# Moving the two additions behind each Strassen group of the down projection from GpSimd to VectorE, in a decoder block on one core

## The chip, the cores and the metric

The kernel runs on one core of one Trainium2 chip. The metric is the device time of one execution in microseconds (us); lower is better. The kernel before has a median of 2799.49 us over three runs.

## The reference

The reference is one decoder layer on 512 tokens of width 2048 in float32: a sparse-attention and pooling mixer, a 4-head cross-attention into 256 memory tokens, and a dense SwiGLU feed-forward network, each between two normalisations. The change touches only the last part:

```python
h = rms_norm(x, ln_ffn_pre[l])
y = (jax.nn.silu(h @ w_gate[l]) * (h @ w_up[l])) @ w_down[l]
x = x + rms_norm(y, ln_ffn_post[l])
```

The hidden width of the network is 5632, that is 44 blocks of 128 rows; `w_down` brings them back to 2048 columns.

## The kernel before

**Precision by splitting.** Every float32 matrix product is made of three TensorE products: an operand x is split in a rounded part hi (ScalarE, L96) and a rest lo = x - hi (VectorE, L97), and `mm3` multiplies hi by hi (L112), hi by lo (L113) and lo by hi (L114). Each weight block thus goes through a pipeline before TensorE can use it: a DMA issued by SyncE into a ring of 4 buffers `wraw`, then the split into a ring of 3 buffers `whi` and one of 3 buffers `wlo`. A `wraw` buffer is free for the next DMA when L97 has read it; a `wlo` buffer when TensorE has used it.

**The down projection.** The output y is held transposed, as 16 tiles `ys` of 128 rows by 512 tokens in SBUF. The 44 blocks of the hidden width are taken in slices. For s = 0 and s = 1 there is a plain slice of 4 blocks (function `down`, whose results are copied into `ys` by ScalarE at L1050 or added to it by VectorE at L1052), and then a slice of 12 blocks that is multiplied by Strassen's method. A last plain slice follows (`half0`, `half1`), and the final normalisation and output.

**A Strassen group.** For each s, eight groups j = 0 to 7 are made, and group j gives the two row tiles `ys[j]` and `ys[j + 8]`. A group calls `strassen` with six sources of 4 x 128 weight columns. For each source, SyncE issues the load (L947), VectorE makes two of the sums of weight blocks (L948: 128 columns, L949: 256 columns), GpSimd makes a third (L950: 128 columns), ScalarE makes `whi` (L96, 896 columns) and VectorE `wlo` (L97, 896 columns). TensorE then makes seven products of 256 columns, three matmuls each: 21 matmuls for a source, 126 for a group. The product into `psO` comes first for every source but a group's first, so a late `wlo` shows at L114 of `psO`. When the six sources are done, ScalarE copies `psO` (L961) and VectorE makes the four result sums from PSUM into the tile `e` (L963, L964 and L965 with 512 columns, L966 with 256).

**Behind the group** stand the two additions of the change, at L1063: 512 columns of `e` each, added to `ys[j]` and to `ys[j + 8]`, with all operands in SBUF. At j = 3 the activations of the next plain slice are loaded and split (two or more L97 of 512 columns on VectorE), ordered behind the last VectorE and ScalarE instruction traced so far (L1059). After the eighth group, `late` takes the last VectorE and ScalarE instruction; the splits of the Strassen operands of s = 1 are ordered behind it (L1054).

**Order.** Each engine runs its instructions in the order in which they are written into its queue. The order is made by a planner before the kernel runs: it plays the program on its own cost model, and takes at each step the ready instruction with the highest priority. Loads and weight preparation (L947 to L951) carry a priority 1000 ahead of their place in the program, the additions at L1063 carry none. Another engine for an instruction can therefore change the order of others.

**The same pattern without GpSimd.** The gate and up projection (f = 4 to 43) uses the same function `strassen` with eight sources for a group. Behind each group VectorE makes two multiplications of 512 columns (`swiglu`, L877 and L879) with both operands in SBUF.

Of the kernel before, what the change touches and what calls it, by code (L numbers as in the profile page):

```python
# [13 lines left out]
ALU = mybir.AluOpType  # L14
# [855 lines left out]
def ffn(net, xctx, xs, xt0, yctx, ys, rb, rf, x2T, second, close):  # L870
    tc, nc, a = net.tc, net.nc, net.a
# [99 lines left out]
    for f in range(NPLAIN, NF):  # L971
        e = strassen(fe, [a["w_gu"][f, j] for j in range(hp)], xops)
# [4 lines left out]
    def act_tile(pool, pair, f, early=EARLY):  # L977
        x0 = pool.tile([P, S], F32, name="a1", bufs=2) if pool is fl else pool.tile([P, 2 * S], F32, name="as", bufs=2)
        x0 = x0[:, :S]
        with tc.high_priority(early):  # L980
            nc.sync.dma_start(x0, actT[f])
            net.split(*pair, x0)
        return pair
# [9 lines left out]
    ys = [fp.tile([P, S], F32, name=f"y{j}") for j in range(KD)]  # L993
# [13 lines left out]
    def operands(i, f):  # L1007

        x = fs.tile([P, 4, 256], F32, name="as", bufs=2)
        nc.sync.dma_start(x[:, 2:4], actT[f].rearrange("p (b c) -> p b c", b=2))  # L1010
        nc.sync.dma_start(x[:, 0:2], actT[f + 1].rearrange("p (b c) -> p b c", b=2))
        net.split(*xq[i], x[:, 0:3])
        t = fs.tile([P, 4, 256], F32, name="t")
        nc.vector.tensor_tensor(t[:, 0:2], x[:, 3:4].broadcast_to([P, 2, 256]), x[:, 1:3], op=ALU.subtract)
        nc.vector.tensor_tensor(t[:, 2], x[:, 1], t[:, 1], op=ALU.subtract)
        nc.vector.tensor_tensor(t[:, 3], x[:, 0], t[:, 2], op=ALU.subtract)
        for k in range(2):
            net.split(tq[i][0][k], tq[i][1][k], t[:, 2 * k:2 * k + 2])
        b = [tuple(v[:, k] for v in xq[i]) for k in (2, 0, 1)]
        return (*b, *[(tq[i][0][k // 2][:, k % 2], tq[i][1][k // 2][:, k % 2]) for k in (1, 2, 0, 3)])  # L1020
# [11 lines left out]
    def down(s, c, act):  # L1032

        ps = [net.psum(("GGSS", "TTSO")[c % 2][d]) for d in range(4)]

        def add(part):
            for f, hi, lo in part:
                for d in range(4):
                    sl = slice(d * P, (d + 1) * P)
                    net.mm3(ps[d], hi[:, sl], lo[:, sl], *act[f], f == 0, f == len(act) - 1)  # L1040
        gemm512(s, c, len(act), [[i] for i in range(len(act) // 2)], add)
        return ps

    f0, late = 0, []
    for s in range(2):
        for c in range(nb):
            for d, ps in enumerate(down(s, c, act)):
                y = ys[4 * c + d]
                if s == 0:
                    nc.scalar.copy(y, ps)  # L1050
                else:
                    nc.vector.tensor_tensor(y, y, ps, op=ALU.add)  # L1052
        f0 += PL
        with net.behind(late):  # L1054
            ops = [operands(i, f0 + 2 * i) for i in range(NS // 2)]
        f0 += NS
        for j in range(hp):
            if j == 3:
                with net.behind(net.last(nc.vector, nc.scalar)):  # L1059
                    act = [act_tile(fs, p, f0 + i, 0) for i, p in enumerate(plain_at)]  # L1060
            e = strassen(fs, [a["w_dst"][s, j, i] for i in range(NS // 2)], ops)
            for k, o in ((j, 0), (j + hp, 5)):
                nc.gpsimd.tensor_tensor(ys[k], ys[k], e[:, o * 256:(o + 2) * 256], op=ALU.add)  # L1063
        late = net.last(nc.vector, nc.scalar)
    sctx.close()

# [47 lines left out]
    for blocks in ((0, 1), (2,), (3,)):  # L1114
        k0, k1 = 4 * blocks[0], 4 * blocks[-1] + 4
        for i, ps in enumerate(half0(2, blocks, act)):
            for j in range(2):
                k = k0 + 2 * i + j
# [53 lines left out]
def body(tc, a):  # L1172
    a = dict(a)
    for n in ("w_cmp", "w_qk", "w_u", "w_z", "w_mix", "w_xq"):
        a[n] = _Halves(a[n])
    for n in ("w_brp", "w_bra"):
        a[n] = _Whole(a[n])
    a["w_down"] = _Down([a[f"w_down{i}"] for i in range(len(SLICES))])
    with ExitStack() as ctx:
        net = Net(ctx, tc, a)  # L1180
        mctx, ms = sublayer1(net)
        st = sublayer2(net, mctx, ms)
        ffn(net, *st)
# [111 lines left out]
```

## Time and profile before

| | us |
|---|---|
| median of three runs | 2799.49 (2798.63 to 2800.45) |
| the profiled execution, its time | 2799.45 |
| the profiled execution, its span in the trace | 2797.7 |
| TensorE busy | 2741.7 (98%) |
| VectorE busy | 2011.7 (72%) |
| GpSimd busy | 612.8 (22%) |

The span runs from the first to the last instruction; the device time is 1.75 us longer. Busy shares are averages over stages with different limits, and the end of a matmul is modelled, so a stop of TensorE is read from the start times of its instructions.

### The profile page before, as it was taken

What the parts mean: (1) busy time and instruction counts of PE and PEld (TensorE: products, weight loads), DVE (VectorE), ACT (ScalarE), POOL (GpSimd) and SP (SyncE); (2) the same over time, 40 slices, a digit from 0 to 9 for tenths busy, and PEclk for the clock granted to TensorE, in tenths of its full rate; (3) what the DMA queues carried; (4) which work ended last, traced back from release to release, by engine and by line L of the source; (5) the groups of instructions that cost most, each with busy time, mean ns of one, the idle gap of its engine ahead of it and who ended that gap; (6) DMA issues with size and microseconds to landing.
All of it is one profiled execution on the core that took longest, in us unless ns stands there. A gap on an engine that the chain in (4) does not pass through costs nothing.

```text
span 2797.7 us, 48879 instructions
## 1 busy us (share of the span) xinstructions
PE 2741.7 (98%) x18384; PEld 2517.8 (90%) x18384; DVE 2011.7 (72%) x3752; ACT 1252.1 (45%) x2061; POOL 612.8 (22%) x715
## 2 busy tenths in 40 slices
PE   9999999999999999999999999999999999999998
PEld 7788887888878889999989999999999999989996
DVE  5655656565645445777798888888988888899756
ACT  4333545454533235654764444444444444343353
POOL 0000000000000000010333444444224223525303
PEclk9999999999999999999999999999999999999999
DMA  6434332333336456763564444444444453444474
GB/s 186 117 101 131 99 96 78 97 97 109 96 105 200 146 154 213 240 214 121 166 203 128 121 118 120 119 121 120 122 115 125 117 170 105 119 136 106 150 247 165
DMA packets 168493, 384.16 MB, mean 137 GB/s; under 512 B 19312, under 2 KB 39840, under 8 KB 168128
## 3 DMA queue, kind: packets, MB, share of 16 engines
q1 hardware_dynamic: 158816, 352.39, 42.1%
q0 software_dynamic: 8864, 27.60, 3.0%
q8 instruction: 144, 2.36, 0.4%
q10 hardware_dynamic: 576, 1.05, 0.1%
q14 instruction: 93, 0.76, 0.1%
HBM read 343.32 MB, written 37.64 MB: 136 GB/s over the span
## 4 chain that ended last, share of the span: by engine, by line
PE 78%; DVE 12%; DMA 6%; issue 2%; ACT 1%; POOL 0%; DVEq 0%; SPq 0%; POOLq 0%; ACTq 0%
PE psG L112 15%; PE psG L114 15%; PE psG L113 15%; DVE wlo L97 5%; PE psS L112 4%; PE psS L113 4%; PE psS L114 4%; PE psT L112 3%; PE psT L114 3%; PE psT L113 3%; DMA wraw<-in_w_dst_dram 3%; DMA wraw<-in_w_gu_dram 2%; PE psO L114 2%; PE psO L112 2%; PE psO L113 2%
## 5 line engine op out<-in xcount | busy, mean ns | idle before, releaser
L96 ACT CAST whi<-wraw 128x896 fp32r<-128x896 f32 (+2 forms) x773 | 758.3, 984 | 1064.1 <-PE psT L114 340.8
L97 DVE TENSOR_TENSOR wlo<-wraw,whi 128x896 fp32r<-128x896 f32 (+2 forms) x773 | 907.4, 1175 | 263.8 <-ACT whi L96 261.0
L950 POOL TENSOR_TENSOR wraw<-wraw 128x128 f32<-128x128 f32 x416 | 415.6, 1001 | 676.1 <-DVE wraw L949 546.9
L112 PE MATMUL psG<-xh,whi 128*128 128x512 f32 (+1 forms) x1072 | 401.0, 374 | 1.6 <-ACT whi L96 1.5
L114 PE MATMUL psG<-xh,wlo 128*128 128x512 f32 (+1 forms) x1072 | 400.1, 373 | 0.8 <-DVE wlo L97 0.8
L113 PE MATMUL psG<-xl,whi 128*128 128x512 f32 (+1 forms) x1072 | 399.7, 373 | 0.0
L112 PEld LDWEIGHTS psG<-xh,whi 128*128 128x128 f32 x1072 | 203.1, 189 | 35.6 <-ACT whi L96 2.9
L114 PEld LDWEIGHTS psG<-xh,wlo 128*128 128x128 f32 x1072 | 202.4, 189 | 33.9 <-DVE wlo L97 1.0
L113 PEld LDWEIGHTS psG<-xl,whi 128*128 128x128 f32 x1072 | 202.8, 189 | 32.5
L948 DVE TENSOR_TENSOR wraw<-wraw 128x128 f32<-128x128 f32 x416 | 137.8, 331 | 103.2 <-DMA wraw<-in_w_gu_dram 67.3
L949 DVE TENSOR_TENSOR wraw<-wraw 128x256 f32<-128x256 f32 x416 | 185.6, 447 | 6.8
L112 PE MATMUL psT<-th,whi 128*128 128x256 f32 x640 | 179.4, 280 | 0.0
L113 PE MATMUL psT<-tl,whi 128*128 128x256 f32 x640 | 178.8, 279 | 0.0
L114 PE MATMUL psT<-th,wlo 128*128 128x256 f32 x640 | 178.7, 279 | 0.0
L114 PE MATMUL psG<-x,wlo 128*128 128x256 f32 (+1 forms) x544 | 158.1, 291 | 3.3 <-DVE wlo L97 3.3
L112 PE MATMUL psG<-x,whi 128*128 128x256 f32 (+1 forms) x544 | 156.8, 288 | 1.5 <-ACT z L764 1.5
L113 PE MATMUL psG<-x,whi 128*128 128x256 f32 (+1 forms) x544 | 157.5, 290 | 0.0
L112 PE MATMUL psG<-mh,whi 128*128 128x256 f32 x512 | 143.4, 281 | 1.1 <-ACT y L630 1.1
L113 PE MATMUL psG<-ml,whi 128*128 128x256 f32 x512 | 143.1, 280 | 0.0
L114 PE MATMUL psG<-mh,wlo 128*128 128x256 f32 x512 | 142.7, 281 | 0.0
L112 PE MATMUL psS<-xh,whi 128*128 128x256 f32 x480 | 134.8, 281 | 1.4 <-ACT xh L99 1.4
L113 PE MATMUL psS<-xl,whi 128*128 128x256 f32 x480 | 135.0, 282 | 0.9 <-DVE xl L100 0.9
(482 smaller groups left out, 7297.2 us busy)
## 6 DMA issues: line engine op xcount, KB each, us to landing
wraw<-in_w_gu_dram SPq DMA_DIRECT2D x320, 256.0 KB, 2.7
wraw<-in_w_z_dram SPq DMA_DIRECT2D x64, 512.0 KB, 3.8
wraw<-in_w_mix_dram SPq DMA_DIRECT2D x64, 512.0 KB, 4.5
wraw<-in_w_down_dram SPq DMA_DIRECT2D x61, 512.0 KB, 5.3
wraw<-in_w_dst_dram SPq DMA_DIRECT2D x96, 256.0 KB, 2.7
wraw<-in_w_gu_dram SPq DMA_DIRECT2D x29, 512.0 KB, 3.7
wraw<-in_w_qk_dram SPq DMA_DIRECT2D x24, 512.0 KB, 3.6
actT<-zs POOLq DMA_DIRECT2D x40, 256.0 KB, 2.3
```

The source lines that it names most:

```text
L96: nc.scalar.copy(hi, x)
L97: nc.vector.tensor_tensor(lo, x, hi.bitcast(F32), op=ALU.subtract)
L112: mm(ps, lh, rh, start=start, stop=False)
L113: mm(ps, lh, rl, start=False, stop=False)
L114: mm(ps, ll, rh, start=False, stop=stop)
L948: nc.vector.tensor_tensor(u[:, 4], u[:, 0], u[:, 3], op=ALU.add)
L949: nc.vector.tensor_tensor(u[:, 5:7], u[:, 0:5:4], u[:, 1:2].broadcast_to([P, 2, P]), op=ALU.subtract)
L950: nc.gpsimd.tensor_tensor(u[:, 7], u[:, 2], u[:, 6], op=ALU.subtract)
```

## The change

Both additions of each of the sixteen groups are issued on VectorE; operands and results stay the same.

```diff
             e = strassen(fs, [a["w_dst"][s, j, i] for i in range(NS // 2)], ops)
             for k, o in ((j, 0), (j + hp, 5)):
-                nc.gpsimd.tensor_tensor(ys[k], ys[k], e[:, o * 256:(o + 2) * 256], op=ALU.add)
+                nc.vector.tensor_tensor(ys[k], ys[k], e[:, o * 256:(o + 2) * 256], op=ALU.add)
         late = net.last(nc.vector, nc.scalar)
```

The instruction that `net.last(nc.vector, ...)` finds at L1059 and L1064 is then the second addition, and no longer L966.

## Rows read from the trace of the kernel before

**Rows 1.** The page's busy times by engine: us, share of the span, instructions.

```profile
PE 2741.7 (98%) x18384; PEld 2517.8 (90%) x18384; DVE 2011.7 (72%) x3752; ACT 1252.1 (45%) x2061; POOL 612.8 (22%) x715
```

**Rows 2.** Stretches: length, then busy PE, PEld, DVE, ACT, POOL; clock, DMA.

```profile
1900.00:2300.00 400.00, 400.00 (x3343) 398.80 (x3342) 349.25 (x594) 168.36 (x204) 136.50 (x175) 1.00 0.44 127
2341.00:2473.00 132.00, 125.86 (x1005) 123.00 (x1005) 114.40 (x171) 51.29 (x63) 67.21 (x58) 1.00 0.44 124
2473.00:2514.00 41.00, 41.00 (x201) 34.73 (x201) 39.96 (x69) 17.96 (x24) 6.91 (x6) 1.00 0.38 111
2514.00:2648.00 134.00, 126.62 (x1034) 124.29 (x1033) 114.17 (x174) 50.64 (x61) 64.58 (x58) 1.00 0.43 117
2648.00:2797.00 149.00, 137.61 (x881) 123.84 (x880) 95.31 (x146) 63.88 (x98) 24.27 (x32) 0.98 0.62 211
```

**Rows 3.** All waits of TensorE, 2341 to 2648 us: total, times, longest.

```profile
PE psO L114 <- DVE wlo L97: 13.4, 15, 1.7
```

**Rows 4.** Timeline of TensorE, stops at `psO`: start, us, instruction, [idle before].

```profile
2360.02 0.39 PE L114 MATMUL psO<-xh,wlo 128*128 128x256 f32 x1 [0.32 <-DVE wlo L97]
...
2406.05 0.39 PE L114 MATMUL psO<-xh,wlo 128*128 128x256 f32 x1 [0.17 <-DVE wlo L97]
...
2441.28 0.28 PE L112 MATMUL psO<-xh,whi 128*128 128x256 f32 x1
2441.40 0.28 PE L113 MATMUL psO<-xl,whi 128*128 128x256 f32 x1
2442.41 0.39 PE L114 MATMUL psO<-xh,wlo 128*128 128x256 f32 x1 [0.73 <-DVE wlo L97]
2442.64 0.28 PE L112 MATMUL psG<-xh,whi 128*128 128x256 f32 x1
...
2518.55 0.39 PE L114 MATMUL psO<-xh,wlo 128*128 128x256 f32 x1 [0.57 <-DVE wlo L97]
...
2633.15 0.39 PE L114 MATMUL psO<-xh,wlo 128*128 128x256 f32 x1 [0.84 <-DVE wlo L97]
```

**Rows 5.** Timeline of VectorE behind one group of the down projection.

```profile
2438.65 0.41 DVE L966 TENSOR_TENSOR e<-psT,e 128x256 f32<-128x256 f32 x1
2438.98 1.27 DVE L948 TENSOR_TENSOR wraw<-wraw 128x128 f32<-128x128 f32 x1
2440.18 2.18 DVE L97 TENSOR_TENSOR wlo<-wraw,whi 128x896 fp32r<-128x896 f32 x1
2442.28 0.41 DVE L949 TENSOR_TENSOR wraw<-wraw 128x256 f32<-128x256 f32 x1
```

**Rows 6.** Timeline of GpSimd, the pairs of additions (each row two instructions).

```profile
2356.42 2.59 POOL L1063 TENSOR_TENSOR y<-y,e 128x512 f32<-128x512 f32 x2 [0.43 <-DVE e L965]
...
2438.81 2.60 POOL L1063 TENSOR_TENSOR y<-y,e 128x512 f32<-128x512 f32 x2 [0.36 <-DVE e L965]
2454.73 2.59 POOL L1063 TENSOR_TENSOR y<-y,e 128x512 f32<-128x512 f32 x2 [0.36 <-DVE e L965]
...
2529.76 2.59 POOL L1063 TENSOR_TENSOR y<-y,e 128x512 f32<-128x512 f32 x2 [0.36 <-DVE e L965]
...
2629.56 2.59 POOL L1063 TENSOR_TENSOR y<-y,e 128x512 f32<-128x512 f32 x2 [0.36 <-DVE e L965]
```

**Rows 7.** Timeline of VectorE behind one group of the gate and up projection.

```profile
2056.88 0.41 DVE L966 TENSOR_TENSOR e<-psT,e 128x256 f32<-128x256 f32 x1
2057.21 0.28 DVE L948 TENSOR_TENSOR wraw<-wraw 128x128 f32<-128x128 f32 x1
2057.41 1.08 DVE L97 TENSOR_TENSOR wlo<-wraw,whi 128x896 fp32r<-128x896 f32 x1
2058.41 0.68 DVE L877 TENSOR_TENSOR zs<-e,rb 128x512 f32<-128x512 f32 x1
2059.02 0.41 DVE L949 TENSOR_TENSOR wraw<-wraw 128x256 f32<-128x256 f32 x1
```

**Rows 8.** Waits of VectorE for reloaded weights, 2341 to 2648 us.

```profile
DVE wraw L948 <- DMA wraw<-in_w_dst_dram: 29.3, 40, 2.8
```

**Rows 9.** Waits of SyncE's queue for buffers, same stretch, the longest row.

```profile
SPq L947 <- DVE wlo L97: 130.4, 65, 4.9
```

**Rows 10.** Timeline of VectorE, a long reload wait in a queue.

```profile
2587.86 1.08 DVE L97 TENSOR_TENSOR wlo<-wraw,whi 128x896 fp32r<-128x896 f32 x1
2590.90 0.29 DVE L948 TENSOR_TENSOR wraw<-wraw 128x128 f32<-128x128 f32 x1 [1.96 <-DMA wraw<-in_w_dst_dram]
```

## The prediction, made before the changed kernel was run

> **What bounds the kernel now.** I read the page first: TensorE is busy for 98% of the span [rows 1], so only its stops can be won back. The view of stretches says where they are. In the gate and up projection TensorE shows no idle time at all; in the two Strassen stages of the down projection it is idle for 132 - 125.86 = 6.1 us and 134 - 126.62 = 7.4 us; the plain slice between them has none [rows 2]. VectorE is busy for about 86% of both kinds of stage, so the busy share alone doesn't say why one stops and the other not.
>
> The view of waits names one thing for all of it: L114 of `psO` waits for `wlo`, 13.4 us in 15 waits [rows 3]. The timeline gives the place. In the steady stream one matmul starts 0.12 us behind the other; at a stop L114 starts 1.01 us behind L113, and the next matmul 0.23 us behind L114, so a stop shown as 0.73 us idle costs 0.89 + 0.11 = 1.00 us [rows 4]. Each stop thus costs its idle time and 0.27 us; all fifteen 13.4 + 15 x 0.27 = 17.5 us. A second reading agrees: from the first to the seventh pair of additions of a stage, six groups, 98.31 and 99.80 us pass [rows 6], and 6 x 126 matmuls at 0.12 us are 90.7 us, so the groups lose 7.6 + 9.1 = 16.7 us.
>
> Thirteen of the fifteen stops stand right behind a pair of additions (the first at 2360.02, the last at 2633.15); the two others, at 2406.05 and 2518.55, don't [rows 4]. VectorE's timeline shows the link. Behind L966 come L948 and the `wlo` that TensorE waits for. They take 1.27 and 2.18 us there, and from the start of L948 to the start of the next instruction 3.30 us pass [rows 5], while GpSimd runs its two additions, 2.60 us from 2438.81 [rows 6]. In the gate and up projection, where GpSimd runs nothing at that point, the same pair takes 2058.41 - 2057.21 = 1.20 us [rows 7]. So the additions on GpSimd hold VectorE up for 3.30 - 1.20 = 2.10 us a group, and the late `wlo` ends 0.05 us before L114 starts.
>
> **The change part by part.**
> *Removed:* 32 additions on GpSimd. GpSimd is not what ends last (it is busy for 67 of 132 us [rows 2]), so its own time counts nothing; what counts is 2.10 us of VectorE in each group.
> *Added:* 32 additions of 512 columns on VectorE with both inputs in SBUF. L877 is the same shape with the same kinds of operands: it is recorded with 0.68 us, and the next instruction starts 0.61 us behind it [rows 7]. A pair thus costs 2 x 0.61 = 1.22 us. It waits for nothing: `e` comes from the same queue, `ys` was last written a stage earlier. Queued behind it are L948, L949 and L97 of the next sources; TensorE waits for them, and SyncE, whose reloads wait for L97 [rows 9].
> *Net on VectorE:* 2.10 - 1.22 = 0.88 us less a group.
> *Where the pair lands* is the planner's choice, and no row shows it. If it stands directly behind L966, the `wlo` ends 0.88 us earlier than now. If it lands as L877 does, behind the next L948 and L97 [rows 7], this `wlo` comes the whole 2.10 us earlier and the 1.22 us fall on the next source. Bounds: 0.88 us a stop below, the whole stop above. I take the lower value as the base, since over a whole group VectorE gains 0.88 us wherever the pair stands, and a queue that runs late from group to group is ruled by that sum.
> *Hidden part:* VectorE waits for reloaded weights at L948, 29.3 us in 40 waits, 1.8 us a group over sixteen [rows 8]. An addition that falls into such a wait costs nothing; it was so for some of GpSimd's time too. I put no number on it.
> *Moved with it:* the splits at j = 3 and those of s = 1 are now ordered behind the second addition and not behind L966: 1.22 us later in the queue, but no longer held up by GpSimd, and inside the sum above. No DMA is added or moved. GpSimd's L950 no longer stands behind the additions; ScalarE's `whi` comes earlier, which no stop waits for.
>
> *Sum:* 13 stops x 0.88 us = 11.4 us. The stop at 2406.05 (0.17 + 0.27 us) and a few shorter ones that the view of waits doesn't count are lateness carried on from the pair before; I add 1.1 us as an estimate. That is 12.5 us. Nothing behind takes it back: the plain slice between the stages runs without a stop, and behind 2648 us TensorE is busy for 137.6 of 149 us, its idle time being the tail of the output [rows 2]. From the profiled execution's own 2799.45 us: 2799.45 - 12.5 = 2787.0 us. The median is 0.04 us off, so the same number holds against it.
>
> Two rules of the Trainium skill bear on it. "SBUF — State Buffer", section "Who interferes with whom", says that a VectorE instruction with two SBUF inputs and a GpSimd instruction that reads SBUF shut each other out for the whole instruction. By that rule the pair would cost VectorE its full 2.60 us, and the change would give 13 x (2.60 - 1.22) = 17.9 us, 2781.5 us, an estimate. The row shows 2.10 us, so the sum stays with the row. "Perfetto Trace Analysis", section "Optimizing Scalar/DVE Operations", speaks against the change: with VectorE saturated, moving work to other engines, even GpSimd, may make sense, though the port they share may undo it. The last rival below is what that would make of this kernel.
>
> **The rivals.**
> *All stops go.* The pair lands behind the urgent `wlo` or in the reload waits. For it: L877 lands so [rows 7], and 2.10 us is more than the longest stop (1.7 us idle and 0.27 [rows 3]). Against: the 1.22 us must still find room, and the two stops not behind a pair stay. At the most 17.5 us: 2782.0 us.
> *Another wait takes its place.* The planner's new order puts L948 of a source directly behind the L97 that frees its buffer, as at 2587.86, where VectorE then stands still for 1.96 us [rows 10]; the mean reload wait is 29.3 / 40 = 0.73 us [rows 8]. Each such place costs 1.23 us more. Eight of sixteen groups with one more would eat 9.8 of the 12.5 us: 2796.8 us. Against: in the trace such a long wait is rare. It would be slower than before only from eleven such groups on.
> *Slower: VectorE becomes the bound.* If what stretches L948 and L97 were not the additions but something that stays, the pair would add 1.22 us to every late `wlo`: 13 x 1.22 = 15.9 us, 2815.3 us. It decides if L948 and L97 still take more than 2.1 us together behind the new additions (3.30 less 1.22). Against it: the stretch starts and ends with the pair of additions [rows 5, 6], and is absent in the other stage with the same code [rows 7].
>
> **How the numbers follow.** A measurement of this kernel can tell about 0.2%, 5.6 us, from no change. The base case has a chance of 0.60, own range 2782 to 2791.5 us; all stops gone (or a better order on top) 0.17; another wait in its place 0.15, counted as no change; slower 0.08, two thirds of it VectorE as the bound and the rest a much worse order. The predicted time is the base case's, 2787.0 us. For eight in ten, the range reaches below the case of all stops gone, to 2780, and up to the case of another wait, to 2797. Faster by over 0.2%: 0.60 + 0.17 = 0.77, less 0.01 for a base case that falls short; within 0.2%: 0.16; slower by over 0.2%: 0.08.
>
> **What would show it.** L1063 on VectorE with about 0.68 us; L948 and L97 behind a group back at 0.28 and 1.08 us; TensorE's wait for `wlo` in the two stages down from 13.4 us to some 3 us; six groups in 93 to 95 us in place of 98 to 100; the stretches after 2648 us of the same length, only earlier. The prediction is wrong if L948 and L97 stay stretched, if the additions themselves take clearly more than 0.7 us, if waits for reloaded weights grow well above 29 us, or if the time is lost again behind the stages.

## The result, and the profile after

| | us | against the kernel before |
|---|---|---|
| kernel before, first pair of runs | 2799.06 (2798.39 to 2800.45) | |
| changed kernel | 2783.59 (2781.71 to 2786.87) | 0.9947 [0.9931, 0.9962], 15.5 us less |
| changed kernel, second time | 2778.77, before 2796.26 | 0.9937 [0.9924, 0.9949], 17.5 us less |
| changed kernel, third time | 2781.08, before 2796.35 | 0.9944 [0.9927, 0.9961], 15.3 us less |

Each time is set against the kernel before in runs of the same occasion (medians 2795.3 to 2799.1 us). The change makes the kernel 15 to 17.5 us faster. The forecast was 12.5 us less, 2787.0 us; the direction and the place are as forecast, the gain is larger than its sum.

The page's busy times of the changed kernel, and its stretches (length, then busy PE, PEld, DVE, ACT, POOL; clock, DMA share, GB/s), beside [rows 1, 2]:

```profile
PE 2738.6 (98%) x18384; PEld 2517.6 (90%) x18384; DVE 2013.0 (72%) x3784; ACT 1250.4 (45%) x2061; POOL 510.7 (18%) x683
```

```profile
2341.00:2473.00 132.00, 131.83 (x1021) 128.13 (x1021) 116.79 (x200) 54.11 (x67) 41.53 (x41) 1.00 0.44 132
2473.00:2514.00 41.00, 40.12 (x239) 35.72 (x238) 35.67 (x62) 16.69 (x22) 7.76 (x8) 1.00 0.40 116
2514.00:2640.00 126.00, 124.17 (x1018) 122.43 (x1018) 106.93 (x185) 49.90 (x61) 41.70 (x40) 1.00 0.46 132
2640.00:2782.00 142.00, 130.06 (x807) 116.08 (x805) 89.58 (x140) 58.70 (x92) 24.23 (x32) 0.97 0.60 205
```

In the first Strassen stage TensorE now stands still for 0.2 us where it stood still for 6.1 us [rows 2], in the second for 1.8 us where it was 7.4 us. VectorE took over 32 instructions and is yet busy for less: from 1 us ahead of the first of the sixteen L966 to 6 us behind the last, its busy time falls by 12.0 us, first before, then after:

```profile
2355.20:2649.48 294.28, 280.76 (x2130) 269.31 (x2129) 258.37 (x396) 114.57 (x142) 134.29 (x118) 1.00 0.43 121
2350.35:2632.52 282.17, 279.29 (x2133) 269.45 (x2133) 246.38 (x427) 113.22 (x142) 87.75 (x86) 1.00 0.43 126
```

The page's total hides this (2011.7 us before, 2013.0 us after): a second profile of the same kernel before has 2031.1 us there, nearly all of the difference ahead of these stages.

TensorE's and VectorE's waits in the two Strassen stages of the changed kernel (total, times, longest), beside [rows 3, 8]:

```profile
PE psO L114 <- DVE wlo L97: 2.5, 3, 0.9
```

```profile
DVE wraw L948 <- DMA wraw<-in_w_dst_dram: 17.0, 24, 2.2
DVE wlo L97 <- ACT whi L96: 14.3, 17, 1.3
```

The wait of TensorE falls from 13.4 us in 15 to 2.5 us in 3. VectorE waits less for reloaded weights than before (29.3 us in 40 waits [rows 8]; 22.8 us in 39 in a second profile of the kernel before).

The view of line L1063 and VectorE's timeline behind one group of the changed kernel, beside [rows 5]:

```profile
L1063 DVE TENSOR_TENSOR y<-y,e x32: 680/687/958, 2352.9 to 2627.4; 128x512 f32<-128x512 f32 x32
```

```profile
2428.84 0.42 DVE L966 TENSOR_TENSOR e<-psT,e 128x256 f32<-128x256 f32 x1
2429.17 0.28 DVE L948 TENSOR_TENSOR wraw<-wraw 128x128 f32<-128x128 f32 x1
2429.37 0.69 DVE L1063 TENSOR_TENSOR y<-y,e 128x512 f32<-128x512 f32 x1
2429.97 1.09 DVE L97 TENSOR_TENSOR wlo<-wraw,whi 128x896 fp32r<-128x896 f32 x1
2430.97 0.69 DVE L1063 TENSOR_TENSOR y<-y,e 128x512 f32<-128x512 f32 x1
2431.57 0.42 DVE L949 TENSOR_TENSOR wraw<-wraw 128x256 f32<-128x256 f32 x1
```

L948 and L97 are back at 0.28 and 1.09 us, and the additions take 0.69 us. In this group they stand neither both ahead of the urgent `wlo` nor both behind it: one is ahead, one behind. It is so in nine of the fourteen groups that have a next one in their stage; in the other five both stand behind it. Two distances in this timeline carry the rest of this document. From the start of L948 to the start of L949 VectorE needs 2.40 us where it needed 3.30, that is 0.90 us less. But from the start of L966 to the end of the urgent `wlo` it is 2431.06 - 2428.84 = 2.22 us where it was 2442.36 - 2438.65 = 3.71 us [rows 5], that is 1.49 us less.

Not all of the difference between the two profiled executions is the change's. The first Strassen group of the down projection starts at 2336.62 us before and at 2332.18 us after, 4.44 us earlier, although every queue runs the same order up to there; the twelve other profiled executions of this study, the kernel before among them, start it between 2331.31 and 2334.59 us. From that start to the end of the span it is 461.06 us before and 449.94, 444.59 and 447.99 us in the three executions of the changed kernel; in the second profile of the kernel before it is 459.32 us. That is 9.4 to 16.5 us less.

### The profile page after: what moved, and what is told of

It reads as the page before. It is cut to its first block, busy times and chain, and to the rows that moved or that the text cites. A ratio compares the mean times of both kernels' runs of the same rounds, so it can differ in the third digit from the quotient of the medians.

```text
span 2782.1 us, 48875 instructions
## 1 busy us (share of the span) xinstructions
PE 2738.6 (98%) x18384; PEld 2517.6 (90%) x18384; DVE 2013.0 (72%) x3784; ACT 1250.4 (45%) x2061; POOL 510.7 (18%) x683
## 4 chain that ended last, share of the span: by engine, by line
PE 88%; DVE 7%; DMA 3%; issue 1%; ACT 1%; POOL 0%; SPq 0%; DVEq 0%; ACTq 0%; POOLq 0%
PE psG L112 16%; PE psG L114 16%; PE psG L113 16%; PE psS L112 5%; PE psS L114 5%; PE psS L113 5%; PE psT L112 4%; PE psT L114 4%; PE psT L113 4%; DVE wlo L97 3%; PE psO L114 2%; PE psO L112 2%; PE psO L113 2%; PE psT L542 1%; DMA wraw<-in_w_dst_dram 1%
## 5 line engine op out<-in xcount | busy, mean ns | idle before, releaser
L97 DVE TENSOR_TENSOR wlo<-wraw,whi 128x896 fp32r<-128x896 f32 (+2 forms) x773 | 900.8, 1167 | 268.8 <-ACT whi L96 264.4
L950 POOL TENSOR_TENSOR wraw<-wraw 128x128 f32<-128x128 f32 x416 | 362.2, 873 | 767.1 <-DVE wraw L949 630.3
L114 PE MATMUL psG<-xh,wlo 128*128 128x512 f32 (+1 forms) x1072 | 399.7, 373 | 0.8 <-DVE wlo L97 0.8
L113 PE MATMUL psG<-xl,whi 128*128 128x512 f32 (+1 forms) x1072 | 399.6, 373 | 0.0
L114 PEld LDWEIGHTS psG<-xh,wlo 128*128 128x128 f32 x1072 | 202.2, 189 | 33.8 <-DVE wlo L97 1.0
L113 PEld LDWEIGHTS psG<-xl,whi 128*128 128x128 f32 x1072 | 202.3, 189 | 32.4
L948 DVE TENSOR_TENSOR wraw<-wraw 128x128 f32<-128x128 f32 x416 | 133.2, 320 | 76.5 <-DMA wraw<-in_w_gu_dram 51.3
L949 DVE TENSOR_TENSOR wraw<-wraw 128x256 f32<-128x256 f32 x416 | 183.5, 442 | 6.1
L114 PE MATMUL psT<-th,wlo 128*128 128x256 f32 x640 | 178.9, 279 | 0.0
L113 PE MATMUL psT<-tl,whi 128*128 128x256 f32 x640 | 178.8, 279 | 0.0
L114 PE MATMUL psG<-x,wlo 128*128 128x256 f32 (+1 forms) x544 | 158.9, 292 | 2.5 <-DVE wlo L97 2.4
L113 PE MATMUL psG<-x,whi 128*128 128x256 f32 (+1 forms) x544 | 158.3, 291 | 0.0
L113 PE MATMUL psG<-ml,whi 128*128 128x256 f32 x512 | 143.1, 280 | 0.0
L114 PE MATMUL psG<-mh,wlo 128*128 128x256 f32 x512 | 142.8, 281 | 0.0
L522 ACT ACTIVATE pr<-pr,mx 128x128 f32<-128x128 f32 (+7 forms) x192 | 90.4, 472 | 102.0 <-DVE mx L518 101.5
L113 PE MATMUL psS<-xl,whi 128*128 128x256 f32 x480 | 134.6, 281 | 1.4 <-DVE xl L100 1.4
```

What stands on the lines that cost most here:

```text
L97: nc.vector.tensor_tensor(lo, x, hi.bitcast(F32), op=ALU.subtract)
L113: mm(ps, lh, rl, start=False, stop=False)
L114: mm(ps, ll, rh, start=False, stop=stop)
L522: nc.scalar.activation(o_, o_, AF.Exp, bias=mx[:, c:c + 1], scale=-1.0, accum_out=sm[:, c:c + 1])
L948: nc.vector.tensor_tensor(u[:, 4], u[:, 0], u[:, 3], op=ALU.add)
L949: nc.vector.tensor_tensor(u[:, 5:7], u[:, 0:5:4], u[:, 1:2].broadcast_to([P, 2, P]), op=ALU.subtract)
```

## The experiments

**The kernel before once more**, for what chance does.

> The kernel before, unchanged, profiled once more. Three theories are tested in these runs. Hold: GpSimd's two additions keep VectorE from its two-input instructions, 2.10 us a group. Occupied GpSimd: what the additions delay is GpSimd's own next work (L950), whatever they read. Order: the planner's new order of VectorE's queue gives the gain. All three expect this run at 2799 us (2797 to 2801), some 13.4 us of waits for wlo in 15 waits, and L948 and L97 behind a group at 1.27 and 2.18 us. Open is only where the first Strassen group of the down projection starts: 2336.6 us in the first profile of the kernel before, 2332.2 us in that of the changed kernel, though nothing ahead of it was changed. If that is chance of one execution, this run starts it anywhere from 2331 to 2338 us; if it belongs to the program, at 2336 to 2337 us.

Measured: 2795.94 us against 2796.38, ratio 1.0 [0.999, 1.0009]. TensorE's wait in the Strassen stages, in a view like [rows 3]:

```profile
PE psO L114 <- DVE wlo L97: 12.1, 15, 1.7
```

The stops belong to the kernel, fifteen of them again; the early start (2332.50 us) doesn't belong to the change.

**No additions at all**, with the order of VectorE's other instructions in these stages as in the kernel before.

```diff
-                nc.gpsimd.tensor_tensor(ys[k], ys[k], e[:, o * 256:(o + 2) * 256], op=ALU.add)
+                pass
```

> The 32 additions of L1063 are left out altogether, so the Strassen parts of the down projection are missing from the output. In both Strassen stages VectorE's queue then has the order of the kernel before. Hold: the stops go without any price on VectorE, 2780 to 2784 us, at most 3 us below the changed kernel; L948 and L97 at 0.28 and 1.08 us. Occupied GpSimd: the same. Order: the order is the old one, so the stops stay, 2797 to 2800 us.

Measured: 2777.19 us, ratio 0.9929 [0.9914, 0.9944], 19.2 us less. TensorE's waits have no row for `wlo` in these stages any more. VectorE's timeline behind a group:

```profile
2427.07 0.27 DVE L948 TENSOR_TENSOR wraw<-wraw 128x128 f32<-128x128 f32 x1
2427.39 1.09 DVE L97 TENSOR_TENSOR wlo<-wraw,whi 128x896 fp32r<-128x896 f32 x1
2428.39 0.42 DVE L949 TENSOR_TENSOR wraw<-wraw 128x256 f32<-128x256 f32 x1
```

The pairs on GpSimd thus cost the kernel before 19.2 us, through VectorE, in an order that doesn't stop TensorE by itself. The same pairs on VectorE cost only 19.2 less 15.3 to 17.5, that is some 2 to 4 us, although sixteen of them occupy it for 16 x 1.22 = 19.5 us.

**A reading GpSimd beside the changed kernel**: each addition is followed by one on GpSimd that reads two parts of `e` and writes a third that nothing needs any more.

```diff
                 nc.vector.tensor_tensor(ys[k], ys[k], e[:, o * 256:(o + 2) * 256], op=ALU.add)
+                nc.gpsimd.tensor_tensor(e[:, 512:1024], e[:, 0:512], e[:, 1280:1792], op=ALU.add)
```

> The changed kernel, and behind each of its additions GpSimd makes an addition of the same shape on parts of e that are no longer used, so it reads and writes SBUF as the old ones did; in the Strassen stages VectorE's queue has the order of the changed kernel. Hold: VectorE pays both, 2.10 us of hold and 1.22 us of additions a group; 13 x 1.22 = 16 us above the kernel before, 2815 us (2807 to 2820), with waits for wlo of 25 us or more. Occupied GpSimd: GpSimd is as busy as before and no more, so about 2799 us. Order: the order is the changed kernel's, so about 2784 us.

**A GpSimd that only writes**, in the same place, with the same order in every queue of these stages:

```diff
                 nc.vector.tensor_tensor(ys[k], ys[k], e[:, o * 256:(o + 2) * 256], op=ALU.add)
+                nc.gpsimd.memset(e[:, 512:1024], 0.0)
```

> As the run before, but GpSimd fills the unused 512 columns of e with zeros (a memset) in place of adding: it only writes SBUF and reads nothing. The order in every queue is the changed kernel's. Hold, if it comes from reading: as the changed kernel, 2782 to 2787 us, L948 and L97 at 0.28 and 1.08 us. Hold, if writing does it too: between 2790 and 2815 us by the memset's length. Occupied GpSimd: slower than the changed kernel by what the memsets last, some 2790 us or more, through late L950, with VectorE's L948 not stretched. Order: 2784 us.

Measured: reading, 2810.53 us, ratio 1.0047 [1.0032, 1.0061], 14.2 us more than the kernel before; only writing, 2778.96 us, ratio 0.9936 [0.9921, 0.995], 17.4 us less. VectorE and GpSimd behind one group, first with the reading GpSimd:

```profile
2440.16 0.28 DVE L948 TENSOR_TENSOR wraw<-wraw 128x128 f32<-128x128 f32 x1
2440.36 0.68 DVE L1063 TENSOR_TENSOR y<-y,e 128x512 f32<-128x512 f32 x1
2440.97 2.18 DVE L97 TENSOR_TENSOR wlo<-wraw,whi 128x896 fp32r<-128x896 f32 x1
2443.07 1.77 DVE L1063 TENSOR_TENSOR y<-y,e 128x512 f32<-128x512 f32 x1
2444.77 0.41 DVE L949 TENSOR_TENSOR wraw<-wraw 128x256 f32<-128x256 f32 x1
```

```profile
2440.32 3.97 POOL L1064 TENSOR_TENSOR e<-e 128x512 f32<-128x512 f32 x2 [0.69 <-DVE e L966]
```

then with the GpSimd that only writes:

```profile
2426.95 0.28 DVE L948 TENSOR_TENSOR wraw<-wraw 128x128 f32<-128x128 f32 x1
2427.15 0.68 DVE L1063 TENSOR_TENSOR y<-y,e 128x512 f32<-128x512 f32 x1
2427.75 1.08 DVE L97 TENSOR_TENSOR wlo<-wraw,whi 128x896 fp32r<-128x896 f32 x1
2428.75 0.68 DVE L1063 TENSOR_TENSOR y<-y,e 128x512 f32<-128x512 f32 x1
2429.35 0.42 DVE L949 TENSOR_TENSOR wraw<-wraw 128x256 f32<-128x256 f32 x1
```

```profile
2426.76 1.11 POOL L1064 MEMSET e<- 128x512 f32 x2 [0.34 <-DVE e L965]
```

TensorE's waits for `wlo` come back with the reading GpSimd, 19.7 us in 24, fewer than the 25 us and more that were expected. Under the reading GpSimd L97 takes 2.18 instead of 1.08 us and the second addition 1.77 instead of 0.68: the hold is back, 2.19 us in all. Under two memsets of the same size no instruction of this group is longer on VectorE than it is alone. So it is not just any instruction on GpSimd that holds VectorE, nor the new order, which is the same in both; it is a GpSimd that reads SBUF. (The memsets are shorter, 1.11 us for the two; but they run beside L948 and the first addition, and neither is stretched.) "SBUF — State Buffer" in the Trainium skill, section "Who interferes with whom", says just this: reads of GpSimd contend with a VectorE instruction that has two SBUF inputs, writes alone don't. The runs agree. They also show GpSimd held in its turn: its two additions took 3.97 us here and 2.60 us in the kernel before [rows 6].

**Half of the change**: only the addition to `ys[j + 8]` is made by VectorE.

```diff
-                nc.vector.tensor_tensor(ys[k], ys[k], e[:, o * 256:(o + 2) * 256], op=ALU.add)
+                (nc.vector if o else nc.gpsimd).tensor_tensor(ys[k], ys[k], e[:, o * 256:(o + 2) * 256], op=ALU.add)
```

> Of the two additions only the second (into the tile j + 8) is moved to VectorE, the first stays on GpSimd. Hold: half the hold and half the price; each is half of the net 0.88 us a group, so 5 to 9 us below the kernel before, with one stretched instruction (about 1.05 us more) behind a group in place of two. Occupied GpSimd: GpSimd is free again 1.3 us earlier, so some half too, but with no stretched instruction. Order: the order is neither the old nor the new one; anything from 0 to 16 us.

Measured: 2786.86 us, ratio 0.9964 [0.9951, 0.9978], 9.4 us less, about half. TensorE's wait, and the two additions side by side on VectorE and GpSimd:

```profile
PE psO L114 <- DVE wlo L97: 6.6, 11, 1.4
```

```profile
2431.43 1.80 DVE L1063 TENSOR_TENSOR y<-y,e 128x512 f32<-128x512 f32 x1
2433.16 1.08 DVE L97 TENSOR_TENSOR wlo<-wraw,whi 128x896 fp32r<-128x896 f32 x1
```

```profile
2431.39 1.30 POOL L1063 TENSOR_TENSOR y<-y,e 128x512 f32<-128x512 f32 x1 [0.69 <-DVE e L966]
```

One addition on GpSimd holds one instruction of VectorE, here the other addition: 1.80 - 0.68 = 1.12 us. Splitting a pair over the two engines makes VectorE's addition wait for GpSimd's, which takes its usual 1.30 us. The stops shrink by more than the 0.37 us that VectorE wins in the group shown (see the table below). In this kernel the planner also put three matmuls between L113 and L114 at the place of the stops in twelve groups, 0.36 us more for the `wlo`; the two together would give about the time won. That is an estimate; no run separates them.

**The pair twice on VectorE**, for whether VectorE has room to spare.

```diff
                 nc.vector.tensor_tensor(ys[k], ys[k], e[:, o * 256:(o + 2) * 256], op=ALU.add)
+                nc.vector.tensor_tensor(e[:, 512:1024], e[:, 0:512], e[:, 1280:1792], op=ALU.add)
```

> The changed kernel with two more additions of 512 columns on VectorE behind each group (on parts of e that are no longer used), and nothing on GpSimd. It prices VectorE's time. If VectorE's time adds up over a group, as the base of the prediction has it, 1.22 us more a group cost 13 x 1.22 = 16 us: about the time of the kernel before. If the additions fall into waits for reloaded weights, 0 to 6 us above the changed kernel.

Measured: 2795.04 us, ratio 0.9996 [0.9987, 1.0005], 16.3 us above the changed kernel measured beside it (2778.77). The second pair costs much of its full length, 16 x 1.22 = 19.5 us, and about the 16 us expected if VectorE's time adds up. But the planner's order changes with it, and TensorE's largest wait is now for `whi`:

```profile
PE psO L112 <- ACT whi L96: 4.8, 2, 3.1
PE psO L114 <- DVE wlo L97: 2.3, 3, 1.7
```

A part of the 16.3 us is TensorE's clock. Behind its stops of 1.67, 1.72 and 3.12 us the granted clock is 0.56, 0.50 and 0.50 for 3.1 to 3.6 us each, the lower of its two levels (1.2 and not 2.4 GHz); the last of the three stretches:

```profile
2564.20:2567.30 3.10, 3.10 (x16) 3.10 (x16) 3.10 (x4) 2.41 (x4) 0.00 (x0) 0.50 0.33 85
```

In the three TensorE made 53 matmuls in 9.9 us, 3.5 us more than at 0.12 us each. And VectorE still waits in the two stages, 21.2 us for `whi` and 9.9 us for reloaded weights. So this run shows the price of more work on VectorE in this planner's order, not that VectorE alone exacts it, nor that it has no room left.

**L950 moved to VectorE as well** in the down projection's groups (96 subtractions of 128 columns, 0.28 us each there), for whether GpSimd's remaining reads cost something too.

```diff
-                nc.gpsimd.tensor_tensor(u[:, 7], u[:, 2], u[:, 6], op=ALU.subtract)
+                (nc.vector if len(srcs) < hp else nc.gpsimd).tensor_tensor(u[:, 7], u[:, 2], u[:, 6], op=ALU.subtract)
```

> The changed kernel, and in the two Strassen stages of the down projection L950 (128 columns, 96 times) also on VectorE, so that GpSimd does nothing there. Hold: L950 holds VectorE too, for some 0.3 us where they meet (L949 0.64 to 0.68 in place of 0.42 us), and on VectorE it costs 0.20 us start to start. Six a group: 1.2 us of price against some 1 us of hold, so within 4 us of the changed kernel either way. If VectorE has room, the shorter way from L949 to whi helps a little.

Measured: 2782.39 us, ratio 0.9946 [0.9931, 0.9961], 3.6 us above the changed kernel beside it, with intervals that overlap. Nothing more is to be had that way in the planner's order, which changed with it.

**Both additions forced ahead of the urgent `wlo`**, by ordering the next splits, and from j = 3 on also L948 and L949, behind the second addition.

```diff
-                nc.vector.tensor_tensor(u[:, 4], u[:, 0], u[:, 3], op=ALU.add)
...
-                net.split(hi[:, 1:8], lo[:, 1:8], u[:, 1:8])
+                with net.behind(after if j >= 3 else []):
+                    nc.vector.tensor_tensor(u[:, 4], u[:, 0], u[:, 3], op=ALU.add)
...
+                with net.behind(after if j >= 1 else []):
+                    net.split(hi[:, 1:8], lo[:, 1:8], u[:, 1:8])
```

Here `after` holds the last two additions. The lines behind it move, so L948 is L951, L966 is L970 and L1063 is L1067.

> The changed kernel, but each pair of additions is forced to stand directly behind L966, ahead of the L97 that TensorE waits for (the splits of the next sources, and the L948 and L949 from j = 3 on, are ordered behind the second addition; this puts two L97 ahead of the next two L948). If where the pair lands is what gave more than 0.88 us a stop, the urgent wlo now ends only 2.10 - 1.22 = 0.88 us earlier than in the kernel before, as the forecast's base case had it: a part of TensorE's waits for wlo comes back (some 3 to 6 us of 12 to 13 us), and the time is 3 to 6 us above the changed kernel. If the landing doesn't matter, because the wlo is in time either way, the waits stay at 1 to 3 us and the time is that of the changed kernel within 2 us.

Measured: 2805.64 us, ratio 1.0033 [1.002, 1.0045]: 9.3 us more than before, 24.6 us above the changed kernel beside it (2781.08). VectorE behind one group, and TensorE's waits:

```profile
2439.31 0.42 DVE L970 TENSOR_TENSOR e<-psT,e 128x256 f32<-128x256 f32 x1
2439.64 1.28 DVE L1067 TENSOR_TENSOR y<-y,e 128x512 f32<-128x512 f32 x2
2440.84 2.09 DVE L97 TENSOR_TENSOR wlo<-wraw,whi 128x896 fp32r<-128x896 f32 x2
2442.85 0.49 DVE L951 TENSOR_TENSOR wraw<-wraw 128x128 f32<-128x128 f32 x2
```

```profile
2441.99 0.39 PE L114 MATMUL psO<-xh,wlo 128*128 128x256 f32 x1 [0.17 <-DVE wlo L97]
...
2448.59 0.39 PE L114 MATMUL psO<-xh,wlo 128*128 128x256 f32 x1 [1.31 <-DVE wlo L97]
```

```profile
PE psO L114 <- DVE wlo L97: 18.5, 26, 2.0
```

Neither theory gave the size, and the run can't decide between them, because the constraint did more than it was meant to. In the kernel before and in the changed kernel the `wlo` behind a pair is that of the fourth source of the group that TensorE is already working on. Here the next splits wait for the additions, so it is that of the second source, which TensorE reaches 42 matmuls, 5.0 us, earlier. TensorE stops for it in thirteen of fourteen groups: 5.35 us in eleven, although it ends only 2.61 us after L966 starts (2441.92, the first of the two L97 taken as 1.08 us, less 2439.31), and 3.85 us in the two groups behind which the activations are split, where it ends 3.82 us after. The other 9.3 us of waits, like that at 2448.59, come in the middle of a group, where L948 and L949 now stand in twos behind two L97.

**TensorE's order put back.** The two orders also differ on TensorE: where the stops are, at the fourth source of a group, L114 of `psO` stands directly behind L113 in ten of the sixteen groups of the kernel before [rows 4]; in the changed kernel the planner put three matmuls between them there in nine groups, which alone gives the `wlo` 0.36 us more. The next two kernels order the other products behind the three matmuls of `psO`, the first for the second source of a group, the other for every source from the second on.

```diff
-                net.mm3(ps, hi[:, blk], lo[:, blk], xh, xl, first and opens, last and closes)
+                with net.behind(head if len(srcs) < hp and j == 1 and ps is not p1 else []): net.mm3(ps, hi[:, blk], lo[:, blk], xh, xl, first and opens, last and closes); head = net.last(nc.tensor) if ps is p1 else (None if first else head)
```

The other kernel has `j >= 1` in place of `j == 1`.

> The changed kernel with TensorE's order behind a group put back: in the down projection's Strassen stages, the other products of the second source (j = 1) are ordered behind the three matmuls of psO. In the kernel before, L114 of psO stands directly behind L113 of psO there; in the changed kernel the planner put three matmuls of psG and psS between them in ten groups, which gives the wlo 3 x 0.12 = 0.36 us more. If this new order of TensorE is what the gain has over 0.88 us a stop, it gives back about 10 x 0.36 = 3.6 us and waits for wlo come back (some 4 to 6 us in all). If the place of the additions is enough by itself, since the wlo ends some 0.6 us ahead of L114 in the changed kernel, of which 0.3 us would be left, it stays within 2 us of the changed kernel, with waits of 1 to 3 us.

> As the kernel with the order put back for the second source, but for every source from the second on, so that no matmul of another product stands between the three of psO anywhere in these stages (the kernel before has such places too, where VectorE waits for reloaded weights). If TensorE's order matters, this gives back 3.6 us and more, up to 8 us; if it doesn't, within 2 us of the changed kernel.

Measured: 2779.78 us, ratio 0.9948 [0.9934, 0.9962], and 2780.78 us, ratio 0.995 [0.9938, 0.9963], against 2795.33: 15.6 and 14.6 us less; TensorE waits for `wlo` not at all in the one and 1.3 us in the other. The first of the two kernels doesn't ask the question: at the second source the changed kernel has L114 directly behind L113 in fourteen of the sixteen groups anyway, and at the fourth source three matmuls still stand between them in ten. The second does: there L114 stands directly behind L113 at the fourth source of all sixteen groups. Its 14.6 us are 0.7 to 2.9 us short of the changed kernel's 15.3 to 17.5 us, measured on other occasions, and not the 3.6 to 8 us that were expected if TensorE's order made the gain. VectorE's queue changed a little in both as well. So TensorE's order explains little of the gain, if any.

**The changed kernel again**, two more times.

> The changed kernel once more, beside the kernels of this call. Hold: 14 to 17 us below the kernel before; from the first Strassen group of the down projection to the end 444 to 450 us (459 to 461 us in two profiles of the kernel before), so that 10 to 16 us of the gain are made in the changed part, and that group starts at 2331 to 2337 us by chance, in which the two kernels don't differ. If a fixed part of the gain came from ahead of the change, that start would be at 2332 us or earlier here too and the gain behind it about 11 us.

> The changed kernel once more, on the same chip as the kernel with the additions forced first. If the 15.5 us and 17.5 us measured so far are one effect with chance of execution on top, it gives 14 to 19 us less than the kernel before; if the first measurement was the true one and the second chance, 15 us or less.

Measured: 17.5 and 15.3 us less (the table above); TensorE's wait for `wlo` is 1.3 us and 1.2 us, in two waits each.

## Why the forecast came out as it did

**What bounds the kernel, and where the stops are.** Confirmed. The kernel without additions has no stop for `wlo`, so the pairs made the two stops that didn't stand behind one too.

**The hold.** Confirmed by undoing it (2.10 us in the kernel before, 2.19 us with a reading GpSimd, nothing with a writing one). It also did away with the slower rival: L948 and L97 do shrink to 0.28 and 1.09 us. Its time does come, though, when the hold is brought back on top of the moved pair: 14.2 us more than before, near the 15.9 us that it was priced at.

**The price of a pair on VectorE.** 0.69 us an addition, 0.68 us forecast.

**The net of 0.88 us a stop: this is the mis-sized term.** The measure of VectorE's sum was right, 3.30 to 2.40 us from L948 to L949. But a stop ends when the urgent `wlo` ends, and this came earlier by more than the sum. In the table, the distances are those of one group each, from the timeline rows shown above and, for the kernel before, from [rows 5].

| kernel | L948 to L949, us | L966 to end of `wlo`, us | time against before, us |
|---|---|---|---|
| before | 3.30 | 3.71 | 0 |
| changed | 2.40 | 2.22 | -15.3 to -17.5 |
| no additions | 1.32 | 1.74 (L966 at 2426.74) | -19.2 |
| GpSimd only writes | 2.40 | 2.21 (L966 at 2426.62) | -17.4 |
| one moved | 2.93 (2431.23 to 2434.16) | 3.34 (L966 at 2430.90) | -9.4 |
| reading GpSimd beside it | 4.61 | 3.32 (L966 at 2439.83) | +14.2 |
| additions forced first | | 2.61, but the `wlo` of another source | +9.3, order changed |

In the kernel before, L114 starts 0.05 to 0.07 us after the end of this `wlo` in all fourteen groups that have a next one: the `wlo` decides. In the three executions of the changed kernel L114 starts 0.30 to 1.26, 0.30 to 2.85 and 0.06 to 1.60 us after it: it is early in all but two groups of the third. The group shown is a common one (2.22 us in seven of the fourteen), but the groups differ. From L966 to the end of the `wlo` 3.67 to 4.91 us pass before and 1.41 to 3.28 us in the first execution after, 0.48 to 2.69 us less in the same group, and in thirteen of the fourteen at least 1.19 us less. What this is worth can be estimated from the timelines, each group taken for itself. In the kernel before the `wlo` came 0.31 to 1.82 us too late (the idle time before L114 and 0.16 us, the part of the 0.27 us that lies ahead of L114), 15.0 us in all. Taking 0.88 us off each leaves 4.0 us of it; taking off what each group's `wlo` really gained leaves 0.2 us. The 3.8 us between the two are about what the forecast fell short by.

The forecast named this landing as its upper bound and took the lower, with the reason that a queue which runs late from group to group is ruled by the sum. As far as these rows show, that reason is the step that failed: VectorE isn't short of time over a whole group. It waited for reloaded weights already in the kernel before [rows 8], and with the hold gone it waits 17.0 us for them and 14.3 us for `whi` in the two stages, some 2 us a group. An addition that stands behind the urgent `wlo` can fall into such time, and leaving both additions out brought only some 2 to 4 us more.

Three things keep this from being shown. The distance from L966 is not TensorE's deadline, since L966 itself moves against TensorE's work: in the third execution of the changed kernel a `wlo` 2.34 us behind L966 stopped TensorE for 0.12 us, and one 3.46 us behind it came 0.73 us early. The reason does seem to hold where VectorE has more to do: with the reading GpSimd the `wlo` lands earlier than in the kernel before in nine of the fourteen groups, and the kernel is still 14.2 us slower, with the longer sum. And the run that was to move the landing alone moved another source's `wlo`. That the landing is the cause of the missing 3 to 5 us is thus argued from rows, not tested.

**The splits at j = 3** were forecast behind the second addition, 1.22 us later. In both stages they stand ahead of it and behind the urgent `wlo`; in the kernel before they stood ahead of that `wlo` and were held too. First before, then after:

```profile
2388.63 3.38 DVE L97 TENSOR_TENSOR x<-as,x 128x512 fp32r<-128x512 f32 x2
2392.13 1.08 DVE L97 TENSOR_TENSOR wlo<-wraw,whi 128x896 fp32r<-128x896 f32 x1
```

```profile
2383.66 1.09 DVE L97 TENSOR_TENSOR wlo<-wraw,whi 128x896 fp32r<-128x896 f32 x1
2384.67 1.29 DVE L97 TENSOR_TENSOR x<-as,x 128x512 fp32r<-128x512 f32 x2
2385.87 0.69 DVE L1063 TENSOR_TENSOR y<-y,e 128x512 f32<-128x512 f32 x1
```

The `wlo` of these two groups won the most, 2.7 us each, and the forecast had no term for it.

**The stops as a sum.** The other route of the forecast, idle time and 0.27 us for each stop, gives the measured size: 17.5 us before, 2.5 + 3 x 0.27 = 3.3, 1.3 + 2 x 0.27 = 1.8 and 1.2 + 2 x 0.27 = 1.7 us after, a gain of 14.2 to 15.8 us. With the second profile of the kernel before, 12.1 + 15 x 0.27 = 16.2 us, it is 12.8 to 14.4 us. So the rival with all stops gone (2782.0 us) was the nearer one; it was given 0.17.

**The rule of the Trainium skill that gave 17.9 us** ("SBUF — State Buffer", section "Who interferes with whom") came near the largest measurement, but not for the step by which it was worked out: VectorE was held for 2.10 us, not for GpSimd's whole 2.60. The first addition of the pair began while L966, which reads PSUM, was still on VectorE, and the hold runs only from the start of VectorE's next instruction. The advice on a saturated VectorE in "Perfetto Trace Analysis", section "Optimizing Scalar/DVE Operations", was no guide to the change: with 86% busy VectorE was partly busy being held. Its caution that the shared port may undo such a move is what these runs show.

**Another wait in its place.** It didn't come: reload waits fell from 29.3 us in 40 (22.8 us in 39 in the second profile) to 17.0 us in 24, the longest from 2.8 to 2.2 us.

**The six groups and the rest.** From the first to the seventh L966 of a stage 92.50 and 94.34 us pass in the changed kernel (forecast 93 to 95, so one a little less; 98.31 and 99.80 between the pairs before):

```profile
2351.35 0.42 DVE L966 TENSOR_TENSOR e<-psT,e 128x256 f32<-128x256 f32 x1
...
2443.85 0.42 DVE L966 TENSOR_TENSOR e<-psT,e 128x256 f32<-128x256 f32 x1
...
2519.78 0.41 DVE L966 TENSOR_TENSOR e<-psT,e 128x256 f32<-128x256 f32 x1
...
2614.12 0.42 DVE L966 TENSOR_TENSOR e<-psT,e 128x256 f32<-128x256 f32 x1
```

From the first transposes of the output to the end of the span it is 155.43 us before and 156.82, 155.05 and 157.17 us after: nothing is taken back behind the stages.

## What to carry to other kernels

An instruction on GpSimd that reads SBUF isn't off the path because GpSimd is idle enough: count its length against VectorE's two-input instructions beside it, and compare that with its price on VectorE; here 2.10 us of hold stood against 1.22 us of work. When a wait ends on one urgent instruction, ask what the new order puts ahead of it, and in how many groups, before taking the queue's sum over a group as the measure: an engine that has waits of its own can take some work behind the urgent instruction at little cost. Such room needn't last: the first pair cost some 2 to 4 us, the second 16.3 us, in another order and with a slower TensorE for a part of it. And check in the trace which instruction a forced order has made the urgent one.

## What was not expected of the hardware

Two executions with the same order in every queue can be 4.4 us apart before they reach the changed place, so one pair of traces is to be compared from that place on. A GpSimd memset of 128 x 512 took 0.53 us on the mean and left VectorE untouched, while an addition of the same size on GpSimd took 1.30 us and held it for 1.1 us. And the hold works both ways: GpSimd's two additions took 3.97 us in place of 2.60 us where VectorE had more two-input work.
